# Output projection with tokens on the partitions, in a two-layer encoder with window and differential attention

## The chip, the core and the metric

The kernel runs on one core of one Trainium2 chip. The metric is the time of one execution on the device in microseconds (us). All matrix work is float32 in the reference; the kernel splits each operand into a high part `hi` (rounded to the matmul type fp32r) and a rest `lo`, and makes one product out of three: hi·hi, lo·hi and hi·lo.

## The reference

Two sequences pass through the same two layers: 1024 prompt tokens and 512 sample tokens, each with 16 meta tokens in front, so 1040 and 528 tokens, 1568 in all, of D = 1024 values. A layer is (cut, with `rmsnorm(x, g) = x * rsqrt(mean(x*x) + EPS) * g`):

```
def layer(x, cos, sin, w_in, w_out, pre_g, post_g, ...):
    h = rmsnorm(x, pre_g)
    aq, ak, av, ag, bq, bk, bv, bg = split(h @ w_in)        # 3328 columns
    oa = window_gqa_attention(rope(aq), rope(ak), av, sink) * silu(ag)   # 512 wide
    ob = rmsnorm(diff_attention(rope(bq), rope(bk), bv, lam), subln_g) * (1 - lambda_init) * silu(bg)   # 512 wide
    o = concat([oa, ob]) @ w_out                            # 1024 x 1024
    return x + rmsnorm(o, post_g)
```

After the second layer the meta tokens are cut off; 1536 tokens go out.

## The kernel before

Everything lies with the model's dimension on the partitions ("dims on partitions"): x, the normed h and the projections are tiles of 128 dims by tokens. The 1568 tokens are cut into four chunks of 392 (`CH`); `dense` multiplies a stationary 128x128 block of weights by the 392 tokens of a chunk and adds up over the depth in a PSUM tile `ps_d`, of which there are two. The attention output ("mix") goes to DRAM as `MX` and comes back in halves of 512 dims: half `FH` is complete early (window attention), the other only at the layer's end.

Every operation is first recorded and then placed on its engine's queue by a list scheduler (`schedule`, L329). It has cost constants of its own and a priority for each operation, which is its number in the program less a boost and a base. So the order on an engine is not the order of the code, and nearly all instructions carry the line of the helper that emits them (L451). An operation written as `any_copy` or `any_tt` goes to the engine that the scheduler finds free first.

The output projection of layer l (`outproj`, L1306) runs in steps that a string per layer lists (`O0`, `O1`; a letter, then chunks):

- `b` (`first`): load the early half of mix (`load_mix`, which also splits it into hi and lo), multiply by half of `w_out`, copy the results from PSUM to `part`. It lies beside attention.
- `s` and `S` (`second`): the other half; VectorE adds `ps_d` to `part`, ScalarE squares the sums, and the squares are added up over the eight blocks of 128 dims (`squares`).
- `f` (`fetch`): load x. `p` (`post`): inverse root of the mean square (`rstd_bc`), post gain, residual sum, store to `X1` (layer 0) or to the output. In layer 0 also the statistics of the new x (`prestats`).
- `n` (`pre`, `prenorm`): pre gain times x times inverse root, split in hi and lo, which is the input `hT` of layer 1's projection (`inproj`, `project`).

With dims on the partitions a sum over dims crosses partitions. `rstd_bc` (L693) does it so: TensorE transposes the sums of squares into a `ps_t` tile, VectorE reduces along the free axis into a small tile `sm`, GpSimd makes the power −1/2 there, and TensorE spreads `sm` over 128 partitions by a second transpose, from which a copy makes `rb` [128 x tokens]:

```
nc.tensor.transpose(pt[0:m, 128 * j:128 * j + 128], acc[:, o:o + m], ident)
...
nc.gpsimd.tensor_tensor(col[0:m, ja:jb], col[0:m, ja:jb], mhalf[0:m, ja:jb], op=ALU.pow)
...
nc.tensor.transpose(pb[:, o:o + m], col[0:m, j:j + 1].to_broadcast([m, 128]), ident[0:m, 0:m])
```

Names in the rows: `ps_d` is the PSUM tile of dense products, `ps_s` of scores, `ps_o` of value products, `ps_t` of transposes; `whl` is a weight split in hi and lo (some lie in `vv` or `kk`, pools of attention that are free by then), `slot` and `pp` are large working tiles (mix, part, x, h), `ru`, `t`, `at` smaller ones.

Of the kernel before, what the change touches and what calls it, by code (L numbers as in the profile page):

```python
# [21 lines left out]
D = 1024  # L22
# [10 lines left out]
ICH = [[(0, 392)], [(392, 392)], [(784, 256), (1056, 120)], [(1176, 392)]], [[c] for c in CH]  # L33
OCH = [
    [[c] for c in CH],
    [[(16, 384)], [(400, 384)], [(784, 256), (1056, 128)], [(1184, 384)]],
]
SEQ = [(0, LP), (LP, LS)]
# [6 lines left out]
O0 = "b0123 f1 S01 s23 f0 p0 p1 n0 f2 p2 f3 n1 n2 p3 n3"  # L45
O1 = "b0123 s0 s2 s1 f1 s3 f2 f0 p1 p2 p0 f3 p3"
# [6 lines left out]
STORE = ((2, 2, 2, 2), (4, 4, 2, 1))  # L53
# [5 lines left out]
PRE_ACT = ((0, 0, 0, 0, 0, 0, 0, 0), (1, 1, 1, 1, 1, 1, 1, 1))  # L59
POST_ACT = ((0, 0, 0, 0, 0, 0, 0, 0), (1, 0, 1, 0, 1, 0, 1, 0))  # L60
# [67 lines left out]
PE_SWITCH = 0.39  # L128
POOL_MAX = 300
# [109 lines left out]
class Recorder:  # L239
# [89 lines left out]
    def schedule(self):  # L329
# [16 lines left out]
        def push(o):  # L346
            for e in o.alts:
                heapq.heappush(ready[e], (o.prio, o.seq, o))
# [194 lines left out]
def hymba_kernel(ctx, tc, xT, w_in, w_out, rope, masks, pre_g, post_g, sub_g, sink_b, sink_m, lam_in, yT):  # L543
# [97 lines left out]
    postg = const.tile([128, NL, 8], F32, name="postg")  # L641
    dma(postg, post_g)
# [33 lines left out]
    X1 = dr.tile([128, 8, T], F32, name="X1")  # L676
# [75 lines left out]
    def prenorm(l, ci, xs, rb, n):  # L752
        his, los = [], []
        for i in range(2):
            hi, lo = pair(F32R)
            for j in range(4):
                r = slice(j, j + 1)
                h = at_p([128, 1, CN])
                scaled(h, xs[i][:, r], preg[:, l, 4 * i + j:4 * i + j + 1], rb, n, PRE_ACT[l][2 * ci + i])
# [10 lines left out]
    def load_w(src, pool=None, pri=0):  # L770
        nc.boost = BOOST_W + pri * 100000
        nc.extra = [after[0]] if pool and after else []
        raw = (p_p if pri else wraw_p)([128, 1024])
# [71 lines left out]
    def project(l, e, w, ci, early):  # L845
# [5 lines left out]
        if l == NL - 1 and ci == 0 and k in ("aq1", "aq2", "gate"):  # L851
            segs = [(META, segs[0][1] - META)]
            hi, lo = [x[:, META:] for x in hi], [x[:, META:] for x in lo]
# [432 lines left out]
    def load_mix(l, ci, half, small=False):  # L1286
# [3 lines left out]
        n = sum(m for _, m in OCH[l][ci])  # L1290
        for r0 in range(4 * half, 4 * half + 4, k):
            hi, lo = [p_p([128, 2, CN], F32R) for _ in range(2)] if small else pair(F32R)
            o = 0
            nc.extra = [after[0]] if small else []
            for (t0, m) in OCH[l][ci]:
                dma(lo[:, :, o:o + m], SC[l]["MX"][r0:r0 + k, :, t0:t0 + m].rearrange("e p t -> p e t"))
                o += m
# [6 lines left out]
        return rows(his, k), rows(los, k), n  # L1304

    def outproj(l):  # L1306
        part, mix, accs, kept = {}, {}, {}, {}
        src = xT.rearrange("(a p) t -> p a t", p=128) if l == 0 else X1
        dst = X1 if l == 0 else yT.rearrange("(a p) t -> p a t", p=128)

        def first(*cs_):
            for ci in cs_:
                mix[ci] = load_mix(l, ci, FH[l])
                part[ci] = pair()
# [10 lines left out]
        begun = {}  # L1325

        def squares(ci, d, od, n):
            acc = accs[ci][0]
            if d == 0:
                nc.scalar.activation(acc[:, 0:n], od, AF.Square)  # L1330
                begun[ci] = nc.last
            else:
                nc.extra = [begun[ci]]
                sq = ru_p([128, 2, CN])[:, 0]
                nc.scalar.activation(sq[:, 0:n], od, AF.Square)
                nc.extra = []
                nc.any_tt(acc[:, 0:n], acc[:, 0:n], sq[:, 0:n], ALU.add)

        def second(*cs_, keep=True):
            for ci in cs_:  # L1340
                mix[ci] = load_mix(l, ci, 1 - FH[l], ci == 3)
                accs[ci] = t1_p([128, CN]), mix[ci][2]
            for dp in range(4):
# [4 lines left out]
                else:  # L1348
                    w = kept[dp]
                for ci in cs_:  # L1350
                    hi, lo, n = mix[ci]
                    for d in (2 * dp, 2 * dp + 1):
                        ps = dense(wrows(w, 4 * (d % 2), 4), hi, lo, n, keep and SPARE[1])
                        od = part[ci][d // 4][:, d % 4, 0:n]
                        nc.boost = BOOST_S
                        nc.vector.tensor_tensor(od, od, ps[:, 0:n], op=ALU.add)
                        nc.boost = 0
                        squares(ci, d, od, n)

        def full(*cs_):  # L1360
            for ci in cs_:
                hb, lb, n = load_mix(l, ci, FH[l])
                ha, la, n = load_mix(l, ci, 1 - FH[l], ci == 3)
                mix[ci] = ha + hb, la + lb, n
                part[ci] = pair()
                accs[ci] = t1_p([128, CN]), n
            for dp in range(4):
                wa = load_w(w_out[l, 1 - FH[l], dp], k_p if dp % 2 else None)
                wb = load_w(w_out[l, FH[l], dp], v_p if dp % 2 else None)
                for ci in cs_:  # L1370
# [153 lines left out]
```

## Time and profile before

| | |
|---|---|
| runs of the kernel before | 1966.04, 1966.86, 1968.27 us; median 1966.86 |
| the profiled execution | 1966.48 us; span from first to last instruction 1964.5 us |
| mean granted clock of TensorE | 0.978 of full speed |
| TensorE busy | 1839.0 us, 94% of the span |
| VectorE busy | 1551.5 us, 79% |
| ScalarE busy | 1013.2 us, 52% |
| GpSimd busy | 272.8 us, 14% |

The busy share is a mean over stages with different limits: a stage may be bound by an engine that has the smaller share over the span. The DMA engines moved 271 MB in the span, at a mean of 138 GB/s.

### The profile page before, as it was taken

The numbers are of one execution on the slowest core, as the hardware profiler recorded it, in microseconds if no ns is written. First come the engines' busy times: TensorE is split into PE (matmuls) and PEld (weight loads), VectorE is DVE, ScalarE is ACT, GpSimd is POOL, SyncE is SP. The second block draws the span as 40 slices with busy tenths as digits, with TensorE's granted clock in tenths as the row PEclk, the third lists the DMA queues.
The fourth block names the chain that finished last, engine by engine and source line by source line (L and its number), as shares of the span: only waits on it lengthen the run. The fifth ranks groups of instructions, "written<-read, shape, count | busy, mean of one in ns | idle before, by whom it ended". The sixth has DMA issues, their size and how long they took to land. (4 is left out here: it accounts for less than half of the span.)

```text
span 1964.5 us, 33387 instructions
## 1 busy us (share of the span) xinstructions
PE 1839.0 (94%) x11424; PEld 1751.8 (89%) x11424; DVE 1551.5 (79%) x3384; ACT 1013.2 (52%) x2364; POOL 272.8 (14%) x486
## 2 busy tenths in 40 slices
PE   6999999999999999999687999999999999999995
PEld 5989999999989989998576999999999999889995
DVE  8858788888787797698898596887868859768778
ACT  4335445454454465576445354554545538658642
POOL 3001211211112110010121021011111101100010
PEclk8999999999999999999798999999999999999998
DMA  7253363434443765555343436344463475674444
GB/s 248 58 158 104 113 175 109 135 114 124 139 124 94 165 163 151 134 151 149 133 158 97 151 93 180 99 140 138 109 182 93 120 182 127 168 204 98 127 157 152
DMA packets 289011, 271.05 MB, mean 138 GB/s; under 512 B 91402, under 2 KB 266058, under 8 KB 288714
## 3 DMA queue, kind: packets, MB, share of 16 engines
q1 hardware_dynamic: 288842, 268.92, 48.9%
q8 instruction: 91, 1.49, 0.3%
q14 instruction: 78, 0.64, 0.1%
HBM read 147.43 MB, written 95.94 MB: 124 GB/s over the span
## 5 line engine op out<-in xcount | busy, mean ns | idle before, releaser
L451 PE MATMUL ps_d<-slot,whl 128*128 128x392 f32 (+2 forms) x5712 | 1176.7, 348 | 29.7 <-DVE slot L451 15.4
L451 PEld LDWEIGHTS ps_d<-slot,whl 128*128 128x128 f32 x5712 | 995.6, 191 | 44.4 <-DVE slot L451 19.6
L451 PE MATMUL ps_s<-kk,qq 128*128 128x264 f32 (+9 forms) x1496 | 284.5, 318 | 21.1 <-ACT pp L451 5.4
L451 PE MATMUL ps_o<-at,vv 128*128 128x256 f32 (+6 forms) x1368 | 286.6, 308 | 11.3 <-DVE og L451 4.3
L451 ACT ACTIVATE pp<-ps_s,sm 116x1040 f32<-116x1040 f32 (+4 forms) x208 | 203.8, 980 | 159.7 <-DVE sm L451 152.7
L451 DVE TENSOR_TENSOR at<-ps_t,at 128x256 fp32r<-128x256 f32 (+6 forms) x472 | 224.2, 481 | 71.3 <-ACT at L451 65.1
L451 ACT ACTIVATE at<-ps_t 128x256 fp32r<-128x256 f32 (+9 forms) x435 | 187.8, 440 | 178.4 <-PE ps_t L451 167.3
L451 PEld LDWEIGHTS ps_s<-kk,qq 128*128 128x128 f32 (+4 forms) x1496 | 227.3, 184 | 48.6 <-ACT pp L451 9.6
L451 DVE TENSOR_REDUCE sm<-ps_s 116x1 f32<-116x1040 f32 (+4 forms) x208 | 218.5, 1051 | 43.4 <-PE ps_s L451 42.1
L451 ACT ACTIVATE pp<-pp,sm 128x336 f32<-128x336 f32 (+5 forms) x339 | 200.7, 606 | 85.0 <-DVE sm L451 83.5
L451 PEld LDWEIGHTS ps_o<-at,vv 128*128 128x128 f32 (+1 forms) x1368 | 214.8, 190 | 22.7 <-DVE at L451 7.5
L451 PE MATMUL ps_t<-ident,pp 128*128 128x128 f32 (+4 forms) x1208 | 192.8, 269 | 3.9 <-DVE at L451 2.7
L451 POOL TENSOR_TENSOR pad<-pp,pad 128x64 fp32r<-128x64 f32 (+3 forms) x143 | 47.2, 332 | 790.9 <-ACT pad L451 487.4
L451 PEld LDWEIGHTS ps_t<-ident,pp 128*128 128x128 f32 (+4 forms) x1208 | 142.0, 136 | 16.6 <-DVE at L451 2.6
L451 POOL TENSOR_TENSOR sm<-sm 128x2 f32<-128x2 f32 (+3 forms) x112 | 53.1, 475 | 477.9 <-DVE sm L451 464.4
L451 DVE CUSTOM_DVE_ANT_0 pp<-ps_s,mk,nsinks 128x336 f32<-128x336 f32 (+2 forms) x192 | 97.8, 526 | 17.1 <-PE ps_s L451 15.4
L451 ACT ACTIVATE og<-ps_o 64x128 f32<-64x128 f32 (+4 forms) x248 | 65.9, 287 | 57.8 <-PE ps_o L451 34.2
L451 DVE TENSOR_TENSOR slot<-slot 128x784 f32<-128x784 f32 (+8 forms) x74 | 83.7, 1146 | 7.3 <-ACT slot L451 7.0
L451 DVE TENSOR_TENSOR whl<-wraw,whl 128x1024 fp32r<-128x1024 f32 x62 | 76.5, 1234 | 5.4 <-ACT whl L451 5.0
L451 POOL TENSOR_SCALAR sm<-sm 128x2 f32<-128x2 f32 (+6 forms) x72 | 51.8, 720 | 190.7 <-DVE sm L451 185.8
L451 ACT ACTIVATE pad<-pp 128x64 fp32r<-128x64 f32 (+5 forms) x144 | 33.4, 236 | 82.8 <-DVE pp L451 79.2
L451 ACT ACTIVATE ru<-ps_d 128x392 f32<-128x392 f32 (+3 forms) x93 | 45.6, 490 | 57.6 <-PE ps_d L451 49.3
(145 smaller groups left out, 2055.8 us busy)
## 6 DMA issues: line engine op xcount, KB each, us to landing
wraw<-in_w_in_dram SPq DMA_DIRECT2D x48, 512.0 KB
BS<-st SPq DMA_DIRECT2D x112, 196.0 KB
qq<-qq SPq DMA_DIRECT2D x144, 128.0 KB
qq<-AQ SPq DMA_DIRECT2D x96, 128.0 KB
BV<-st SPq DMA_DIRECT2D x28, 392.0 KB
wraw<-in_w_out_dram SPq DMA_DIRECT2D x20, 512.0 KB
slot<-in_x_dram SPq DMA_DIRECT2D x12, 784.0 KB
GT<-ru SPq DMA_DIRECT2D x48, 196.0 KB
```

The costliest lines, as they stand in the source:

```text
L451: fn(*[_real(a) for a in args], **{k: _real(a) for k, a in kw.items()})
```

## The change

The roles in the output projection's matmuls are swapped. A tile of 128 tokens of mix becomes the stationary operand, and 256 columns of `w_out` move; the result has 128 tokens on the partitions and output dims along the free axis. There are 12 such tiles of 128 tokens (`TILES`, three per chunk of 384), and in layer 0 a thirteenth of 80 rows, "chunk 4", with the two sets of 16 meta tokens and 48 tokens that fill it up; its first half waits in DRAM (`PM`).

What follows works on token tiles: ScalarE squares two halves of 512 with a running sum (`stat`), VectorE adds the two sums, GpSimd makes the power of that one column, the post gain is a multiplication by a tile that holds `post_g` on all partitions (`gains`, step `g`), and the residual sum takes the inverse root as a per-partition scalar. `X1`, the second input `xr` and the output lie token by token in DRAM. For layer 1 the normed x of four token tiles is transposed by TensorE block by block into `ps_t`; `any_copy` with the pre gain makes `hi` from it, and a VectorE operation makes `lo`, both straight from PSUM. `rstd_bc` and `prestats` serve only layer 0's first norm now, `squares` and `full` go. Layer 1's chunks start at token 16, and the meta tokens come last (`ICH[1]`). The step strings change, and with them the order.

```
-O0 = "b0123 f1 S01 s23 f0 p0 p1 n0 f2 p2 f3 n1 n2 p3 n3"
-O1 = "b0123 s0 s2 s1 f1 s3 f2 f0 p1 p2 p0 f3 p3"
+O0 = "b01234 f01 S01 g l2 p0 l3 p1 s4 s2 n0 s3 f4 p4 f2 p2 n1 f3 p3 n2 n3"
+O1 = "b0123 g f0 s0 p0 f1 s1 p1 f2 s2 p2 f3 s3 p3"
...
+        def product(ps, c0, w, m, c, M, behind=()):
+            hi, lo = m
+            for r in range(4):
+                nc.extra = list(behind) if r == 0 else []
+                with nc.macro():
+                    for i, (wt, mt) in enumerate(((0, hi), (1, hi), (0, lo))):
+                        nc.tensor.matmul(
+                            ps[0:M, c0:c0 + 256], lhsT=mt[r][:, c:c + M], rhs=w[:, wt, 2 * r:2 * r + 2],
+                            start=(r == 0 and i == 0), stop=(r == 3 and i == 2))
...
             for dp in range(4):
                 w = load_w(w_out[l, FH[l], dp])
+                u, c0 = dp // 2, 256 * (dp % 2)
                 for ci in cs_:
-                    hi, lo, n = mix[ci]
-                    for d in (2 * dp, 2 * dp + 1):
-                        ps = dense(wrows(w, 4 * (d % 2), 4), hi, lo, n)
+                    for j, (c, M) in enumerate(token_tiles(ci)):
+                        ps = ps_d([128, 512])
+                        product(ps, 0, w, mix[ci], c, M)
                         nc.boost = BOOST_E
-                        nc.any_copy(part[ci][d // 4][:, d % 4, 0:n], ps[:, 0:n])
+                        if ci < 4:
+                            nc.any_copy(part[ci][u][:, j, c0:c0 + 256], ps[:, 0:256])
+                        else:
+                            ev = ru_p([128, 256])
+                            nc.any_copy(ev[0:M], ps[0:M, 0:256])
+                            dma(PM[:, 256 * dp:256 * dp + 256], ev[0:M])
...
-        def squares(ci, d, od, n):
-            acc = accs[ci][0]
...
+            def add(od, ps):
+                nc.boost = BOOST_S
+                nc.vector.tensor_tensor(od, od, ps, op=ALU.add)
+                nc.boost = 0
+
+            if keep:
+                for ci in cs_:
+                    for j, (c, M) in enumerate(token_tiles(ci)):
+                        for u in range(2):
+                            ps = ps_d([128, 512])
+                            w = [get(2 * u + x) for x in range(2)]
+                            done = product(ps, 0, w[0], mix[ci, 1], c, M)
+                            product(ps, 256, w[1], mix[ci, 1], c, M, [done])
+                            add(outs(ci, u, j, M), ps[0:M])
+                        norm(ci, j, M)
...
+        def stat(parts, M):
+            r = sm_p([128, 4])
+            for u, p in enumerate(parts):
+                sq = ru_p([128, 512])
+                nc.scalar.activation(sq[0:M], p, AF.Square, scale=1.0 / 32, accum_out=r[0:M, u:u + 1])
+            nc.vector.scalar_tensor_tensor(
+                r[0:M, 2:3], r[0:M, 0:1], EPS, r[0:M, 1:2], op0=ALU.add, op1=ALU.add)
+            nc.gpsimd.tensor_tensor(r[0:M, 3:4], r[0:M, 2:3], mhalf[0:M, 0:1], op=ALU.pow)
+            return r[0:M, 3:4]
...
-            rb = rstd_bc(acc[:, 0:n], n, 1.0 / D)
-            for u in range(2):
-                for a in (0, 2):
-                    t = oo[u][:, a:a + 2]
-                    scaled(t, t, postg[:, l, 4 * u + a:4 * u + a + 2], rb, n, POST_ACT[l][2 * ci + u])
...
+            for j, (c, M) in enumerate(token_tiles(ci)):
+                for u in range(2):
+                    od, x = outs(ci, u, j, M), xv(ci, u, j, M)
+                    nc.any_tt(od, od, late[0][0:M, u], ALU.mult)
+                    nc.vector.scalar_tensor_tensor(x, od, rs[ci, j], x, op0=ALU.mult, op1=ALU.add)
...
+                if l < NL - 1:
+                    r = stat([xv(ci, u, j, M) for u in range(2)], M)
+                    for u in range(2):
+                        nc.any_copy(xv(ci, u, j, M), xv(ci, u, j, M), r)
...
-                prenorm(l + 1, ci, xin[ci], rbs[ci], accs[ci][1])
...
+                for k in range(4):
+                    d = slice(128 * k, 128 * k + 128)
+                    pt = ps_t([128, 512])
+                    with nc.macro():
+                        for x in range(4):
+                            i = 3 * ci + x
+                            M = 128 if i < 12 else 80
+                            h = xv(i // 3, u, i % 3, M)[:, d]
+                            nc.tensor.transpose(pt[:, 128 * x:128 * x + M], h, ident[0:M, 0:M])
+                    g = preg[:, l + 1, 4 * u + k:4 * u + k + 1]
+                    p = pt[:, 8 * ci:8 * ci + CN]
+                    nc.any_copy(hi[:, k], p, g)
+                    nc.vector.scalar_tensor_tensor(lo[:, k], p, g, f32(hi[:, k]), op0=ALU.mult, op1=ALU.subtract)
```

The first place is TensorE's queue between layer 0's attention and layer 1's first score (`kk`). Before, the last stretch of it is

```order
L451 MATMUL ps_t<-ident,t_10852 98x128 x4
L451 MATMUL ps_d<-slot,whl 128x392 x15
L451 MATMUL ps_t<-ident,sm 128x98 x4
L451 MATMUL ps_d<-pp,whl 128x392 x12
L451 MATMUL ps_t<-ident,slot 98x128 x4
L451 MATMUL ps_d<-pp,whl 128x392 x12
L451 MATMUL ps_t<-ident,sm 128x98 x4
L451 MATMUL ps_d<-pp,whl 128x392 x24
L451 MATMUL ps_d<-slot,kk 128x392 x24
```

After the change the queue behind the last value product (`ps_o`) begins so:

```order
L451 MATMUL ps_o<-at,vv 128x512
L451 MATMUL ps_d<-whl,slot 128x256 x12
L451 MATMUL ps_t<-ident,slot 128x128 x12
L451 MATMUL ps_d<-whl,slot 128x256 x30
L451 MATMUL ps_t<-ident,slot 128x128 x8
L451 MATMUL ps_d<-whl,slot 128x256 x15
L451 MATMUL ps_t<-ident,slot 128x128 x8
L451 MATMUL ps_d<-whl,slot 128x256 x3
L451 MATMUL ps_d<-kk,at 80x256 x12
```

The transposes of `t` and `slot` (sums of squares) and of `sm` (spreading), each with products between, are gone there; transposes of normed tiles (`slot`), 8 to 12 in a row, stand between narrow products of the same projection. In the whole stretch from the last value product to the first score there are 543 wide matmuls and 72 transposes before, and 252 narrow and 399 wide matmuls and 144 transposes after; 249 wide ones stand behind the last transpose of the last chunk, where 150 stood.

The second place is the end of VectorE's queue. Before, its last rows are

```order
L451 SCALAR_TENSOR_TENSOR slot<-slot,postg,rb 128x384 x2
L451 TENSOR_TENSOR slot<-slot,ps_d 128x384 x2
L451 TENSOR_TENSOR slot<-slot 128x4x384
L451 TENSOR_TENSOR t_22663<-t_22663,ru 128x384 x2
L451 TENSOR_REDUCE sm<-ps_t 128x3
L451 TENSOR_TENSOR slot<-slot,rb 128x384 x4
L451 TENSOR_TENSOR slot<-slot 128x384 x4
L451 SCALAR_TENSOR_TENSOR slot<-slot,postg,rb 128x384 x4
L451 TENSOR_TENSOR slot<-slot 128x384 x4
```

and after the change

```order
L451 TENSOR_TENSOR slot<-slot,ps_d 128x512 x2
L451 SCALAR_TENSOR_TENSOR sm<-sm 128x1
L451 TENSOR_TENSOR slot<-slot 128x512
L451 SCALAR_TENSOR_TENSOR slot<-slot,sm 128x512 x2
L451 TENSOR_TENSOR slot<-slot 128x512
L451 TENSOR_TENSOR slot<-slot,ps_d 128x512
L451 SCALAR_TENSOR_TENSOR sm<-sm 128x1
L451 TENSOR_TENSOR slot<-slot 128x512
L451 SCALAR_TENSOR_TENSOR slot<-slot,sm 128x512 x2
```

Behind the last sum with `ps_d` there stand a column addition, a product with the gain (the other half's stands before it or on another engine) and two residual operations of one token tile, where four rows of a whole chunk stood behind a reduction.

## Rows read from the trace of the kernel before

**Rows 1.** The page's busy times: us, share of the span, instructions.

```profile
PE 1839.0 (94%) x11424; PEld 1751.8 (89%) x11424; DVE 1551.5 (79%) x3384; ACT 1013.2 (52%) x2364; POOL 272.8 (14%) x486
```

**Rows 2.** Windows: stretch, length, busy of PE, PEld, DVE, ACT, POOL; clock, DMA.

```profile
897.40:950.40 53.00, 49.41 (x294) 45.86 (x295) 45.42 (x125) 35.79 (x102) 5.38 (x12) 0.94 0.45 130
950.40:1079.00 128.60, 93.81 (x457) 85.44 (x456) 116.88 (x199) 66.05 (x110) 26.27 (x18) 0.84 0.41 135
1079.00:1106.70 27.70, 27.70 (x161) 27.33 (x161) 10.47 (x16) 6.09 (x10) 0.00 (x0) 1.00 0.66 204
1845.00:1855.00 10.00, 9.79 (x69) 9.12 (x69) 9.01 (x34) 8.94 (x28) 1.38 (x3) 1.00 0.48 152
1869.70:1945.20 75.50, 71.27 (x400) 67.75 (x399) 59.81 (x104) 28.05 (x55) 7.28 (x7) 1.00 0.48 159
1945.20:1964.50 19.30, 1.97 (x8) 1.00 (x6) 12.34 (x23) 1.48 (x3) 1.04 (x2) 0.60 0.38 139
```

**Rows 3.** Waits of TensorE, 950.4 to 1079: total us, times, longest.

```profile
PE ps_t L451 <- POOL sm L451: 21.4, 5, 10.5
PE ps_d L451 <- DVE slot L451: 9.8, 7, 3.7
```

**Rows 4.** VectorE's groups by shape, 897.4 to 1079: busy, mean ns | idle before.

```profile
L451 DVE SCALAR_TENSOR_TENSOR slot<-slot,postg,rb 128x392 f32<-128x392 f32 x32 | 19.0, 631 | 2.7 <-ACT rb L451 2.7
L451 DVE TENSOR_TENSOR slot<-slot 128x784 f32<-128x784 f32 x20 | 18.8, 966 | 0.1
L451 DVE TENSOR_TENSOR slot<-at,slot 128x392 fp32r<-128x392 f32 x32 | 17.2, 557 | 0.1
...
L451 DVE TENSOR_TENSOR slot<-slot,ps_d 128x392 f32<-128x392 f32 x28 | 15.2, 555 | 4.1 <-PE ps_d L451 3.3 <-PE ps_o L451 0.7
L451 DVE TENSOR_TENSOR t<-t,ru 128x392 f32<-128x392 f32 x25 | 13.9, 558 | 0.5 <-ACT ru L451 0.3
...
L451 DVE TENSOR_TENSOR slot<-slot 128x1568 f32<-128x1568 f32 x4 | 7.1, 1784 | 0.0
L451 DVE TENSOR_REDUCE sm<-ps_t 98x4 f32<-98x512 f32 x8 | 5.5, 685 | 3.0 <-PE ps_t L451 2.9
...
L451 DVE SCALAR_TENSOR_TENSOR rw<-ps_d,scl,cs 128x392 f32<-128x392 f32 x4 | 2.5, 621 | 0.3 <-PE ps_d L451 0.3
...
L451 DVE TENSOR_TENSOR at<-ps_t,at 128x256 fp32r<-128x256 f32 x2 | 0.8, 424 | 0.0
```

**Rows 5.** TensorE's timeline at two places: start, us, operation, xcount.

```profile
926.35 0.69 PE L451 MATMUL ps_o<-at,vv 128*128 128x256 f32 x4
926.87 0.70 PE L451 MATMUL ps_d<-slot,whl 128*128 128x392 f32 x3
...
996.20 4.53 PE L451 MATMUL ps_d<-pp,vv 128*128 128x392 f32 x24
1000.58 2.92 PE L451 MATMUL ps_d<-slot,whl 128*128 128x392 f32 x15
...
1845.53 1.03 PE L451 MATMUL ps_t<-ident,pp 128*128 128x128 f32 x8
1846.32 1.29 PE L451 MATMUL ps_d<-slot,whl 128*128 128x384 f32 x6
...
1850.10 0.63 PE L451 MATMUL ps_o<-at,vv 128*128 128x256 f32 x4
1850.57 0.44 PE L451 MATMUL ps_t<-ident,pad 128*80 128x128 f32 x4
```

**Rows 6.** Timeline of the end, all engines: start, us, operation [idle before].

```profile
1940.92 4.48 PE L451 MATMUL ps_d<-pp,vv 128*128 128x384 f32 x24 [0.32 <-DVE slot L451]
...
1946.09 0.99 ACT L451 ACTIVATE ru<-slot 128x384 f32<-128x384 f32 x2 [4.19 <-DVE slot L451]
...
1951.24 0.85 POOL L451 TENSOR_TENSOR sm<-sm,mhalf 128x3 f32<-128x3 f32 x1
...
1959.48 1.96 DVE L451 TENSOR_TENSOR slot<-slot 128x384 f32<-128x384 f32 x4
```

More of the change, by code (lines that the diff above doesn't have):

```diff
@@ L675, in hymba_kernel @@
     nc.base = 0
-    X1 = dr.tile([128, 8, T], F32, name="X1")
+    X1 = dr.tile([T, D], F32, name="X1")
+    PM = dr.tile([80, D], F32, name="PM")
     SC = []
@@ L772, in load_w @@
         nc.extra = [after[0]] if pool and after else []
-        raw = (p_p if pri else wraw_p)([128, 1024])
+        raw = (p_p if pri or pool and after else wraw_p)([128, 1024])
         dma(raw, src)
@@ L1347, in second @@
                         kept[dp] = w
-                else:
[L1349 to L1358, printed above, removed]
@@ L1409, in pre @@
-        def pre(ci):
-            if l < NL - 1:
-                prenorm(l + 1, ci, xin[ci], rbs[ci], accs[ci][1])
-        steps = dict(b=first, s=second, S=lambda *c: second(*c, keep=False), F=full, f=fetch, p=post, n=pre)
+                    return w
+                return kept[dp]
+            def add(od, ps):
[12 more added lines that the diff above has]
+                        norm(ci, j, M)
+            else:
+                for dp in range(4):
+                    w = get(dp)
+                    for ci in cs_:
+                        for j, (c, M) in enumerate(token_tiles(ci)):
+                            ps = ps_d([128, 512])
+                            product(ps, 0, w, mix[ci, 1], c, M)
+                            add(outs(ci, dp // 2, j, M)[:, 256 * (dp % 2):256 * (dp % 2) + 256], ps[0:M, 0:256])
+                            if dp == 3:
+                                norm(ci, j, M)
@@ new lines, in norm, with fetch @@
+        def norm(ci, j, M):
+            rs[ci, j] = stat([outs(ci, u, j, M) for u in range(2)], M)
+        xin = {}
+        def fetch(ci):
+            nc.boost = BOOST_M if ci == 4 else 0
+            if ci == 4:
+                nc.extra = [after[0]]
+                xm = p_p([128, 2, 512])
+                o = 0
+                for (t0, m) in OCH[ci]:
+                    dma(xm[o:o + m].rearrange("p u d -> p (u d)"), src[t0:t0 + m])
+                    o += m
+                nc.extra = []
+                xin[ci] = [xm]
+            else:
+                if l == 0 and ci == 3:
+                    xin[ci] = [p_p([128, 2, 512]) for _ in range(3)]
+                else:
+                    xin[ci] = halves([128, 3, 512])
+                nc.extra = [after[0]] if l == 0 and ci == 3 else []
+                for u in range(2):
+                    for j, t0 in enumerate(TILES[ci]):
+                        dma(xv(ci, u, j), src[t0:t0 + 128, 512 * u:512 * u + 512])
+                nc.extra = []
+            nc.boost = 0
@@ L1414, in outproj @@
+        steps = dict(b=first, s=second, S=lambda *c: second(*c, keep=False), f=fetch, p=post, n=pre, l=load, g=gains)
         for step in OUT_ORDER[l].split():
             nc.base = BASE[l].get(step[0], 0)
-            steps[step[0]](*[int(c) for c in step[1:]])
+            for c in ([step[1:]] if step[0] in "bsS" else step[1:] or [""]):
+                steps[step[0]](*[int(x) for x in c])
         nc.base = 0
```

153 lines of the change are left out of this document (71 added, 82 removed).

## The prediction

> **What bounds the kernel now.** I first read the busy shares of the page: TensorE is busy 94% of the span and no other engine is above 79% [rows 1]. So a saving on another engine counts only where TensorE is seen to wait, and the next view to read is busy time by stretch. I cut stretches at marks of the program: the last unit of attention of layer 0 (897.4 to 950.4 us), the turn from there to the last lo part of layer 1's input (950.4 to 1079), the input projection up to layer 1's first score product (1079 to 1106.7), and at the end layer 1's second half of the output projection (1869.7 to 1945.2) and what follows its last matmul (1945.2 to 1964.5) [rows 2].
>
> [...] In the turn TensorE is busy 93.8 us of 128.6, and VectorE 116.9: VectorE is the fuller engine there. [...] And the last 19.3 us hold 8 matmuls: a chain, in which VectorE works 12.3 us. The waits of TensorE in the turn say which: 21.4 us for the small GpSimd tile `sm` (the inverse root, before it is spread over 128 partitions by a transpose), and 9.8 us for VectorE's work on `slot` [rows 3].
>
> How much VectorE work is at stake is read from its groups between 897.4 and 1079 [rows 4]. Seven of them belong to the part that is rewritten, and so do 32 pre-gain products on `at`, as long as the 32 lo operations.
>
> **The change, part by part.** *TensorE.* A 392-wide matmul costs 0.1825 us where 24 follow each other: (1000.58 - 996.20)/24 [rows 5]. For a 256-wide one there are two rows, both of four in attention: 0.1175 (1850.57 - 1850.10) and 0.13 (926.87 - 926.35). The wide rate scaled by columns gives 0.119, which lies at the lower one; I take 0.119 and keep 0.13 as the upper bound, 0.1175 as the lower. A 128x128 transpose costs 0.099 us, (1846.32 - 1845.53)/8.
> - Layer 0: 768 matmuls of 392 columns become 13 token tiles x 96 = 1248 of 256 (the thirteenth tile is the 80 meta and filler tokens): 1248 x 0.119 - 768 x 0.1825 = 148.5 - 140.2 = +8.3 us; about half of it in the first halves under attention, +4.
> - Layer 1: 768 of 384 columns become 1152 of 256: 137.1 - 137.3, nothing. Its input projection has new chunks; 288 matmuls for queries and gates are 16 columns narrower: 288 x 16/392 x 0.1825 = -2.1 us.
> - Transposes: 88 for the norms go (the order lists them), 128 come: +40 x 0.099 = +4.0 us; the 24 that go from the end save 2.4 there, the rest lies in the turn.
>
> *VectorE in layer 0.* By the means of [rows 4] this goes: 32 post-gain products x 0.631, 16 residual sums x 0.966, 28 sums of squares x 0.558, the squares of the new x (1.784 + 0.966 + 0.557 for each of four chunks), eight reductions x 0.685, 64 pre-gain and lo operations x 0.557, 32 sums with PSUM x 0.555: 123 us. This comes: 24 sums with PSUM of 256 (0.424), 20 of 512 (about 0.69, by the slope of 0.409 us between the 392- and the 784-wide sum), 26 gain products of 512 (0.68), 26 residual operations (0.631 + 120 x 0.00104 = 0.76), 32 lo operations from PSUM (0.621), ten hi parts (0.62), and about 10 us of small columns, scaled copies and the fifth chunk: 97 us. Net -26 us. The squares go to ScalarE with a running sum; it is busy 102 us of the 181.6 there [rows 2] and loses its own pre-gain pass, so I cost that at nothing; without that cover each 512-wide square would delay its tile's norm by under 1 us.
>
> *The turn.* VectorE has 162.3 us of work in 181.6 us (897.4 to 1079), 89%. With 136 us at the same 89% the last lo part comes after 153 us, 28.6 earlier. But the new order leaves 249 wide matmuls of the input projection behind the last transposes, 249 x 0.1825 = 45.4 us, where now 27.7 us are left: net -11 us. The other bound is TensorE alone: from attention's last product to the first score it has 252 narrow and 399 wide matmuls and 144 transposes, 30.0 + 72.8 + 14.3 = 117.1 us, for what now takes from 950.4 to 1106.7, 156.3 us: -39. I take -17, near the VectorE end, because VectorE stays the engine that the norms wait for; a little beyond it, because the eight trips TensorE - GpSimd - TensorE go, and with them the 21.4 us in which TensorE stood with ready products behind a transpose.
>
> *Where the stall goes.* VectorE, not TensorE, now waits for `sm`: one column per token tile on GpSimd, 26 times in layer 0. Behind a residual operation that waits stand the sums that free `ps_d`. In the order other tiles' sums stand between, so I add nothing, and this is rival B.
>
> *Narrow products and PSUM.* With half of the depth and 256 columns a `ps_d` tile is full after 12 x 0.119 = 1.43 us instead of 12 x 0.1825 = 2.19, and there are two of them. An eviction costs VectorE 0.424 and must come within that time although VectorE and ScalarE also serve attention. I add 2 us; the bounds are 0 and 10.
>
> *The end.* Now 19.1 us lie between the last dense matmul (1940.92 + 4.48) and the end: sum, squares, transposes, the power on GpSimd, transposes, copy, sixteen VectorE operations of a quarter chunk each, the last at 1959.48 to 1961.44, and 3.1 us for its store [rows 6]. After the change the last matmul is followed by one 512-wide sum (0.69), one square (0.99/2 for 384, so 0.65 for 512) with its running sum (estimate 0.2), a one-column addition (0.2), the power (at most the 0.85 of three columns), two residual operations (1.4) and the store (3.1), with five hand-overs of about 0.2: 8 us. That is -11.
>
> *Sum.* Turn -17, end -11, first halves +4, input projection -2, transposes at the end -2 (inside the -11 chain only in part; I count 1), evictions +2: -25. The profiled run took 1966.5 us (span 1964.5 and 2.0 around it), 0.4 below the median of the runs shown, so this holds for both: **1941 us**.
>
> **Rivals.** *A, TensorE becomes the bound of the turn.* For it: no engine has more than 136 us of work left in what are now 181.6 us, and the waits behind `sm` on TensorE are gone. Against it: 89% is what the fuller engine reaches now. Then -39 instead of -17: 1919.
> *B, the turn gives nothing.* The 26 us come back as VectorE waits on the one-column chain, square, addition, power, and as filled `ps_d`. For it: TensorE waits for VectorE's `slot` already now [rows 3]. Then only the end counts: 1958.
> *C, the narrow products cost more.* Place: all 2400 of them, about 2150 outside the turn's hidden part. At 0.13 the gain is gone by 2150 x 0.011 = 24: 1965, no change. From 0.131 on the kernel is slower, at 0.14 it takes 1986. For it: one of two rows stands at 0.13. Against: the other stands at 0.1175, and the wide rate gives 0.119 by columns alone.
> [...]
> *That the change does nothing* would need C's rate or a turn and an end that both keep their length; I know no row for the second.
>
> **How the numbers follow.** Forecast (1930 to 1952) 0.54; A, 0.15; B (1952 to 1962) 0.18; no change, C at its bound, 0.05; C beyond it 0.04; D 0.04. About 0.2% is what a measurement of this kernel can tell from no change, 3.9 us. Faster: 0.54 + 0.15 + 0.18 = 0.87; same 0.05; slower 0.08. The range for 8 in 10 leaves out no change and both slower cases (0.13) and half of A (0.07): 1920 to 1960.
>
> **What the profile after would show.** VectorE's busy time between the last unit of attention and the last lo part 26 us shorter, and the turn's waits of TensorE for `sm` gone. 256-wide `ps_d` matmuls 0.119 us apart in runs of 12 and more; at 0.13 C is right. [...] First score of layer 1 about 17 us sooner after attention's last product than the 156.3 us of now. Last matmul to end 8 us. I am wrong if VectorE shows new idle time before `slot<-slot,sm`, or `ps_d` waits for ScalarE and VectorE grow under attention by more than 10 us.

## The result and the profile after

The changed kernel takes 1938.49 us (median of four runs, 1930.33 to 1938.88), before it was 1966.45 over the runs on the same chips; the ratio is 0.9852, with a 95% interval of 0.982 to 0.9884. Run again beside the last experiments (e9) it gave 0.9839 (0.9825 to 0.9854); e9's numbers leave out one execution of five, which took 2986 us at a granted clock of 0.56. Forecast were 1941 us, 25 less than before; measured are 28 less. The profiled run took 1938.61, with a span of 1936.8.

The page's busy times after, as in [rows 1]:

```profile
PE 1843.4 (95%) x12328; PEld 1771.3 (91%) x12328; DVE 1515.2 (78%) x3363; ACT 1008.1 (52%) x2417; POOL 279.3 (14%) x516
```

TensorE has 904 more instructions and 4 us more busy time in a span that is 28 us shorter, and VectorE 36 us less. To see where the time went I cut both traces at the same four marks of the program, all read from TensorE's timeline: the start of layer 0's last value product, layer 1's first score product, layer 1's last value product, the end.

| us | to last value product, layer 0 | turn to first score | layer 1 to last value product | to the end | span |
|---|---|---|---|---|---|
| before | 950.1 | 156.6 | 762.8 | 95.0 | 1964.5 |
| after | 960.8 | 136.5 | 749.9 | 89.5 | 1936.8 |
| difference | +10.7 | -20.1 | -12.9 | -5.5 | -27.7 |

The stretches of the changed kernel in windows, columns as in [rows 2]: the last 55 us of layer 0's attention, the first 16.8 us of the turn, the 7 us behind them, the rest up to the last lo part of layer 1's input, the input projection up to the first score, and what follows the last matmul's start.

```profile
905.80:960.80 55.00, 49.94 (x392) 46.84 (x391) 49.91 (x144) 40.69 (x115) 9.82 (x13) 1.00 0.47 130
960.80:977.60 16.80, 4.73 (x28) 3.60 (x26) 14.56 (x33) 11.02 (x27) 7.20 (x9) 0.70 0.67 220
977.60:984.60 7.00, 5.84 (x25) 5.55 (x26) 5.93 (x7) 3.92 (x6) 0.00 (x0) 0.50 0.81 250
984.60:1068.20 83.60, 82.21 (x578) 80.75 (x577) 69.79 (x131) 45.24 (x92) 14.80 (x20) 1.00 0.44 133
1068.20:1097.30 29.10, 29.10 (x172) 28.96 (x171) 5.48 (x9) 5.26 (x10) 0.00 (x0) 1.00 0.62 187
1928.30:1936.80 8.50, 0.28 (x3) 0.07 (x1) 4.06 (x8) 0.72 (x2) 0.92 (x1) 0.81 0.33 123
```

The turn is now two things. For 16.8 us TensorE does almost nothing (4.7 us busy), and the granted clock falls from 1.00 to 0.50 between 967.4 and 967.6. It is still 0.50 in the next 7 us, where 25 narrow products keep TensorE busy for 5.84 us, 0.23 us each; from 984.6 on TensorE is busy 82.2 of 83.6 us at a clock of 1.00, and VectorE, the fuller engine before, 69.8. VectorE's work from 905.8 to 1068.2 is 140.2 us (49.9 + 14.6 + 5.9 + 69.8), where 162.3 stood in [rows 2].

TensorE's waits from 960.8 to 1068, as in [rows 3]:

```profile
PE ps_t L451 <- ACT slot L451: 7.6, 1, 7.6
PE ps_t L451 <- DVE slot L451: 3.5, 1, 3.5
PE ps_d L451 <- DVE slot L451: 1.2, 1, 1.2
PE ps_d L451 <- ACT slot L451: 1.0, 1, 1.0
```

No wait for `sm` is left on TensorE; these four lie in the first 19 us, and the rest of the list adds up to 1.4. VectorE's groups from 905.8 to 1068.2 that took the place of those in [rows 4]:

```profile
L451 DVE SCALAR_TENSOR_TENSOR slot<-ps_t,preg,slot 128x392 fp32r<-128x392 f32 x32 | 19.1, 620 | 3.6 <-ACT slot L451 3.5
L451 DVE TENSOR_TENSOR slot<-slot 128x512 f32<-128x512 f32 x24 | 16.4, 706 | 0.1
L451 DVE SCALAR_TENSOR_TENSOR slot<-slot,sm 128x512 f32<-128x512 f32 x18 | 13.6, 773 | 0.7 <-POOL sm L451 0.7
...
L451 DVE TENSOR_TENSOR slot<-slot,ps_d 128x512 f32<-128x512 f32 x12 | 8.2, 683 | 1.6 <-PE ps_d L451 1.4
L451 DVE TENSOR_TENSOR slot<-slot,ps_d 128x256 f32<-128x256 f32 x16 | 6.6, 414 | 0.7 <-PE ps_d L451 0.7
```

The durations are within 4% of those that were worked out (in the order of the lines 0.621, 0.68, 0.76, 0.69, 0.424), and VectorE waits for `sm` 0.7 us in all. Narrow products in a run and, in the last two lines, wide ones of the input projection, TensorE's timeline, as in [rows 5]:

```profile
993.75 1.58 PE L451 MATMUL ps_d<-vv,slot 128*128 128x256 f32 x12
995.16 1.93 PE L451 MATMUL ps_d<-kk,slot 128*128 128x256 f32 x15
996.93 0.51 PE L451 MATMUL ps_d<-vv,slot 128*128 128x256 f32 x3
...
1068.99 0.70 PE L451 MATMUL ps_d<-slot,kk 128*128 128x392 f32 x3
...
1077.03 0.70 PE L451 MATMUL ps_d<-slot,vv 128*128 128x392 f32 x3
```

(996.93 - 995.16)/15 is 0.118 us for each narrow one; between the last two lines 45 wide ones begin, (1077.03 - 1068.99)/45 = 0.179 us for each, a little under the 0.1825 of [rows 5]. The end, all engines, as in [rows 6]:

```profile
1927.00 1.58 PE L451 MATMUL ps_d<-vv,pp 128*128 128x256 f32 x12
...
1929.51 0.68 DVE L451 TENSOR_TENSOR slot<-slot,ps_d 128x512 f32<-128x512 f32 x1
1930.28 0.63 ACT L451 ACTIVATE ru<-slot 128x512 f32<-128x512 f32 x1 [3.00 <-DVE slot L451]
...
1931.27 0.92 POOL L451 TENSOR_TENSOR sm<-sm,mhalf 128x1 f32<-128x1 f32 x1 [3.73 <-DVE sm L451]
1932.23 1.41 DVE L451 SCALAR_TENSOR_TENSOR slot<-slot,sm 128x512 f32<-128x512 f32 x2 [0.44 <-POOL sm L451]
```

From the end of the last matmul (1927.00 + 1.58) to the end of the span are 8.2 us, where 19.1 stood: one sum, one square, one column through the power, two residual operations, and the store.

### The profile page after: what moved, and what is told of

It is laid out like the page before. It is cut to its first block, busy times and chain, and to the rows that moved or that the text cites. A ratio compares the mean times of both kernels' runs of the same rounds, so it can differ in the third digit from the quotient of the medians.

```text
span 1936.8 us, 35552 instructions
## 1 busy us (share of the span) xinstructions
PE 1843.4 (95%) x12328; PEld 1771.3 (91%) x12328; DVE 1515.2 (78%) x3363; ACT 1008.1 (52%) x2417; POOL 279.3 (14%) x516
## 4 chain that ended last, share of the span: by engine, by line
PE 70%; DVE 11%; DMA 8%; ACT 4%; issue 4%; SPq 2%; POOL 1%; DVEq 0%; POOLq 0%; ACTq 0%
PE ps_d L451 43%; PE ps_s L451 10%; PE ps_o L451 9%; PE ps_t L451 8%; DVE at L451 2%; DVE pp L451 2%; DVE slot L451 2%; ACT pp L451 2%; SPq L451 2%; DVE sm L451 1%; DMA vv<-BV 1%; DVE og L451 1%; DMA kk<-AK 1%; DVE ru L451 1%; POOL sm L451 1%
## 5 line engine op out<-in xcount | busy, mean ns | idle before, releaser
L451 PE MATMUL ps_d<-slot,whl 128*128 128x392 f32 (+2 forms) x4560 | 938.2, 347 | 15.0 <-ACT slot L451 6.7
L451 PEld LDWEIGHTS ps_d<-slot,whl 128*128 128x128 f32 x4560 | 785.7, 190 | 22.2 <-ACT slot L451 6.7
L451 PE MATMUL ps_d<-whl,slot 128*128 128x256 f32 x1800 | 259.0, 288 | 8.6 <-DVE slot L451 6.0
L451 PEld LDWEIGHTS ps_d<-whl,slot 128*128 128x128 f32 x1800 | 235.1, 192 | 14.3 <-DVE slot L451 7.2
L451 ACT ACTIVATE pp<-pp,sm 128x336 f32<-128x336 f32 (+6 forms) x347 | 206.6, 607 | 61.0 <-DVE sm L451 57.6
L451 PEld LDWEIGHTS ps_o<-at,vv 128*128 128x128 f32 (+1 forms) x1368 | 214.0, 190 | 16.8 <-ACT pp L451 5.4
L451 PE MATMUL ps_t<-ident,pp 128*128 128x128 f32 (+6 forms) x1248 | 203.5, 269 | 3.1 <-DVE at L451 1.6
L451 PEld LDWEIGHTS ps_t<-ident,pp 128*128 128x128 f32 (+6 forms) x1248 | 147.8, 137 | 14.7 <-ACT pp L451 2.8
L451 DVE CUSTOM_DVE_ANT_0 pp<-ps_s,mk,nsinks 128x336 f32<-128x336 f32 (+2 forms) x192 | 97.1, 528 | 22.1 <-PE ps_s L451 20.3
L451 POOL TENSOR_TENSOR sm<-sm,mhalf 128x1 f32<-128x1 f32 (+7 forms) x98 | 80.8, 830 | 132.9 <-DVE sm L451 129.6
L451 ACT ACTIVATE ru<-ps_d 128x392 f32<-128x392 f32 (+5 forms) x100 | 48.7, 487 | 73.9 <-PE ps_d L451 64.2
L451 DVE TENSOR_TENSOR slot<-slot 128x512 f32<-128x512 f32 (+3 forms) x79 | 73.9, 945 | 8.4 <-ACT slot L451 8.0
```

Of the source, the lines that this page charges most:

```text
L451: fn(*[_real(a) for a in args], **{k: _real(a) for k, a in kw.items()})
```

## What TensorE waits for at the turn's start

Three lists of the changed kernel belong together. TensorE's timeline:

```profile
961.05 1.59 PE L451 MATMUL ps_d<-whl,slot 128*128 128x256 f32 x12
962.47 0.38 PE L451 MATMUL ps_t<-ident,slot 128*128 128x128 f32 x2
970.42 1.59 PE L451 MATMUL ps_t<-ident,slot 128*128 128x128 f32 x6 [7.57 <-ACT slot L451]
975.50 1.09 PE L451 MATMUL ps_t<-ident,slot 128*128 128x128 f32 x4 [3.49 <-DVE slot L451]
977.60 0.79 PE L451 MATMUL ps_d<-whl,slot 128*128 128x256 f32 x2 [1.01 <-ACT slot L451]
```

the queue that issues the transfers:

```profile
968.73 0.37 SPq L451 DMA_DIRECT2D MX<-og  x1
...
971.08 0.37 SPq L451 DMA_DIRECT2D slot<-MX  x1
971.56 0.44 SPq L451 DMA_DIRECT2D pp<-PM  x1
972.11 1.08 SPq L451 DMA_DIRECT2D pp<-in_w_out_dram  x2
```

and ScalarE's split of the chunk of mix:

```profile
976.06 1.48 ACT L451 ACTIVATE slot<-slot 128x1536 fp32r<-128x1536 f32 x1 [1.28 <-DMA slot<-MX]
```

By name TensorE waits for the norm of a token tile, whose transposes stand at the head of its queue. But the products behind those transposes were not ready either: the last attention result goes to DRAM at 968.7, 7.9 us after its product began, comes back as a chunk of mix from 971.1 on, and the product at 977.6 waits for ScalarE to split it, which ends at 977.5. I call this idle time of TensorE the stand. Two quarters of `w_out` (`pp<-in_w_out_dram`) are asked for only at 972.1, because these loads wait for the last store. The kernel before stood at the same place:

```profile
950.70 2.92 PE L451 MATMUL ps_d<-slot,whl 128*128 128x392 f32 x15
964.11 0.91 PE L451 MATMUL ps_t<-ident,sm 98*128 98x98 f32 x4 [10.50 <-POOL sm L451]
964.73 0.68 PE L451 MATMUL ps_d<-pp,whl 128*128 128x392 f32 x1
```

and ScalarE split the chunk for that last product just ahead of it:

```profile
962.77 0.84 ACT L451 ACTIVATE pp<-pp 128x784 fp32r<-128x784 f32 x1
```

The 10.50 us before 964.11 are half of the 21.4 us that [rows 3] puts down to `sm`. But the split ended only at 963.6, so for all but 0.5 us of them the product behind the transposes was not ready either. The runs e3, e9 and e10 below bear on this.

## Experiments

In each, the rest of the kernel is as before or as changed. Ratios are to the kernel before on the same chip, with 95% intervals. All of them are built by the same list scheduler, so an edit also moves other instructions.

**e1, e2: one layer old, one new.**

```
-        outproj(l)
+        (outproj_b, outproj)[l](l)        # e1: layer 0 old, layer 1 new, residual from xr
+        (outproj, outproj_b)[l](l)        # e2: layer 0 new, layer 1 old, residual from xT
```

> Layer 0 keeps the old output projection and norms (and layer 1 the old chunks), layer 1 has the new ones; layer 1 takes its residual from the kernel's input x instead of layer 0's result, which leaves out one dependency and no work. By stretches of the two traces layer 1's part of the change is 5.5 us after its last value product and 8.5 us ahead of it (12.9 less the 4.4 us of dense work that the new chunks save there). If both belong to layer 1's own steps: 14 us under before, about 1953. If what layer 1 gained under attention came with layer 0's chunks, only 5.5 us: about 1961.

> Layer 0 has the new output projection and norms, layer 1 the old ones, with its residual from the kernel's input x. By stretches layer 0's part is +10.7 us before its last value product, -20.1 in the turn and -4.4 by the new chunks: 14 us under before, about 1953. If layer 1's gain under attention came with layer 0's chunks too: 22 us under, about 1944. The two kernels' gains should add up to the 28 of the whole.

e1 took 1959.52 us, 0.9953 (0.9932 to 0.9974); e2 1943.93, 0.9884 (0.9866 to 0.9903). The gains, 0.47% and 1.16%, add up to 1.63%, the whole change's 1.48% within its interval. They fall nearer to the second expectations. By the four marks:

| us | to last value product, layer 0 | turn | layer 1 to last value product | to the end | span |
|---|---|---|---|---|---|
| e1 | 952.1 | 158.2 | 755.8 | 92.1 | 1958.2 |
| e2 | 960.7 | 136.9 | 758.9 | 85.1 | 1941.6 |

Layer 1's own steps (e1 against before, last two stretches) are worth 762.8 + 95.0 - 755.8 - 92.1 = 9.9 us. In e2 layer 1 has the old steps and is still 762.8 + 95.0 - 758.9 - 85.1 = 13.8 us shorter than before: that came with layer 0's new steps and the new chunks of layer 1's input. Much of it lies early: from the first to the 129th score product of layer 1 there are 121.2 us before, 120.9 in e1, 111.8 in e2 and 112.3 in the changed kernel, 9 us less, ahead of any output projection of layer 1. Not all of that is gained: 27 wide products fewer stand in this stretch (351 where 378 stood, 4.8 us at 0.179), 15 of them now ahead of the first score and 12 behind the 129th. TensorE's idle time in it falls from 3.3 to 0.6 us in the changed kernel.

**e3, e4: the kernel before, without the trip, and with less VectorE work.** e3 leaves out the inverse roots of layer 0's two norms, e4 most of a product with one:

```
-            rb = rstd_bc(acc[:, 0:n], n, 1.0 / D)
+            rb = rstd_bc(acc[:, 0:n], n, 1.0 / D) if l else spread(acc[:, 0:n], n)   # e3: a copy; the same in prestats
...
+                    nc.scalar.activation(h[:, 0, 0:n], xs[i][:, j, 0:n], AF.Copy, scale=g)            # e4
+                    nc.vector.tensor_tensor(h[:, 0, 0:8], h[:, 0, 0:8], rb[:, 0:8], op=ALU.mult)
```

> The kernel before, in which layer 0's two inverse roots per chunk are left out: rb is a copy of the sums of squares themselves, so the transposes, the reduction, the power and the spreading transposes go (64 transposes, eight reductions), and VectorE's other work stays. If VectorE's load bounds the turn, only its 5.5 us of reductions count: about 1960. If it is the trip TensorE - GpSimd - TensorE behind which ready products stand, the 21.4 us of waits for sm go: 1945 or below.

> The kernel before, in which the pre-gain step of layer 1's input multiplies by the inverse root only 8 of 392 columns (the dependence stays, the rest of that product is left out): 32 x about 0.45 = 14 us less VectorE work in the turn, the trips stay. If VectorE's load bounds the turn: 12 to 14 us under before, about 1953. If the trips do: within 4 us of before.

e3 took 1953.94 us, 0.9931 (0.9907 to 0.9956), between its two expectations; its turn is 139.4 us, while its last value product comes at 955.9, 5.8 later than before. e4 took 1952.88, 0.9926 (0.9911 to 0.9942); its turn is 143.2. The turn of e3 in a window, and TensorE's waits in it:

```profile
955.90:1067.50 111.60, 80.70 (x399) 75.01 (x398) 110.88 (x191) 65.54 (x109) 3.46 (x4) 0.88 0.48 156
```

```profile
PE ps_d L451 <- ACT pp L451: 13.2, 1, 13.2
PE ps_d L451 <- DVE slot L451: 11.2, 6, 7.5
```

The same of e4:

```profile
949.70:1065.20 115.50, 88.41 (x460) 81.46 (x459) 107.57 (x211) 60.89 (x99) 19.67 (x18) 0.88 0.45 147
```

Without the trip VectorE works 110.9 of 111.6 us: it is the bound of the old turn, and the trips only added some 12 us in which it stood (128.6 - 116.9 in [rows 2]). In e4 the trips are left. The cut product takes VectorE 3.7 us instead of 17.0; 4.3 of these 13.3 us come back as operations that the scheduler then gave to VectorE. With 9.0 us less busy time of VectorE the turn is 13.4 us shorter (156.6 - 143.2). And without any trip TensorE still stands 13.2 us at the place of the 10.50, now for the split of mix (`ACT pp`), and its waits from the last value product to the first score add up to 30.7 us, where 34.6 stood before. So the trip covered another wait of about the same length.

**e5, e6: the changed kernel with more work for one engine.**

```
+                        nc.vector.tensor_tensor(od, od, od, op=ALU.max)      # e5, layer 0, behind the gain
...
+                            for _ in range(2):                               # e6
                                 nc.tensor.transpose(pt[:, 128 * x:128 * x + M], h, ident[0:M, 0:M])
```

> The changed kernel with one more 512-wide VectorE operation (a maximum of the tile with itself, which changes nothing) for each half of each token tile in layer 0, behind the product with the gain: 26 x 0.68 = 17.7 us more VectorE work, about 14 of them in the turn. In the trace of the changed kernel VectorE works 90 of the turn's 107 us, TensorE stands 15 us at its start and then hardly. If VectorE still bounds the turn: 14 us over the changed kernel, a ratio to before of 0.992. If TensorE does now, behind that one gap: at most 4 us, 0.987.

> The changed kernel with each transpose of a normed tile issued twice: 128 x 0.099 = 12.7 us more TensorE work, of which the 32 of chunk 0 lie in the gap at the turn's start and 96 behind it. If TensorE bounds the turn now: 9.5 us over the changed kernel, ratio to before 0.990. If VectorE does: at most 3 us, 0.987.

e5 took 1955.86 us, 0.9932 (0.991 to 0.9955); e6 1958.91, 0.9945 (0.9924 to 0.9966). By the expectations one of the two additions should have been nearly hidden; neither was. For e6 that agrees with a turn bound by TensorE: its turn is 153.1 us, 16.6 more, of which 12.7 are the transposes and 2.1 are 12 more products of the input projection (12 x 0.179). The rest of its loss lies outside the turn: 2.6 us up to the last value product, and layer 1, which takes 751.9 + 2.1 = 754.0 us with these products added back, instead of 749.9. For e5 it is less plain. Its last value product comes 4.7 us later, though VectorE has only 3 more 512-wide products and maxima ahead of it (14 where 11 stood; in the turn 38 where 15 stood); 9 narrow products more stand there (1.1 us). In the turn 51 wide products more stand ahead of the first score, 9.1 us, so that 153.2 - 9.1 + 1.1 - 136.5 = 8.7 us are longer. TensorE's idle time in the turn is 22.3 us, where 14.6 stood; its longest wait at the start is 11.8 us now, and further on e5's windows are, columns as in [rows 2]:

```profile
984.00:1020.00 36.00, 35.81 (x287) 35.41 (x286) 34.98 (x64) 21.75 (x50) 8.52 (x8) 0.96 0.56 186
1020.00:1050.00 30.00, 24.98 (x144) 23.43 (x143) 26.74 (x53) 18.95 (x39) 6.16 (x8) 0.94 0.39 119
```

VectorE is busy 35.0 of 36 us, and in the 30 us behind them TensorE stands 5. So the added work took up the slack that VectorE has in the changed kernel (69.8 of 83.6 us), and beyond it VectorE is a bound again. And layer 1, which has none of the added work, takes 746.1 + 9.1 = 755.2 us instead of 749.9. e7, e8 and e12, which have the same order of TensorE's instructions in layer 1 as e5, show 753.0 to 754.5 by the same sum, while the changed kernel profiled again (e9) shows 747.8. So 3 to 7 us of e5's loss are the order that the scheduler fell into, and some 12 lie ahead of layer 1, 8.7 of them in the turn.

**e7, e8: the last attention result first.**

```
+        nc.boost = 3000                       # e7, e8: from the copy out of ps_o to the store in MX
...
+            for y in range(0, k, 2 if l == 0 and half == 0 and ci in (2, 3) else k):      # e8: load and split by twos
```

> The changed kernel, in which the operations that bring an attention result from PSUM to DRAM go ahead of all others on their engines (a boost of 3000). In the changed kernel's trace TensorE stands at the turn's start until the last attention result has gone to DRAM and come back as a chunk of mix: 7.7 us from the last value product to its store, because ScalarE and VectorE put norm work between. If that way sets the gap: 3 to 4 us off the gap. If the norms of the first token tiles do (their transposes stand at the head of TensorE's queue): no change or 1 us more.

> As the run before, and the late half of mix of chunks 2 and 3 in layer 0 is loaded and split in two pieces of two heads instead of one of four, so that products can begin on the first piece. If the way of the last attention result sets the gap: another 2 us off it, 5 to 6 in all, ratio to before about 0.983. If the norms do: as the changed kernel, 0.985.

e7 took 1944.92 us, 0.9876 (0.9845 to 0.9908); e8 1945.55, 0.9877 (0.9841 to 0.9913): no gain. From the last value product to the next product that follows the stand there are 15.0 us in e7 (966.66 to 981.66) and 15.7 in e8, instead of 16.8; the store comes 6.1 us after that product in e7 and 8.4 in e8, instead of 7.9. The way was shortened by less than forecast in e7 and its first part not at all in e8, and layer 1's order (3 to 7 us, as in e5) and a last value product that comes 6 us later ate it. Inconclusive as to the rest.

**e9, e10, e11: what the stand is worth.** e9 is the changed kernel again, for the chip. In e10 the loads that waited for the last attention result's store wait for its last value product only:

```
+            read[:] = [nc.last]               # behind the last value product
...
-        nc.extra = [after[0]] if pool and after else []
+        nc.extra = [read[0]] if pool and after else []        # and at the four other places
...
-BASE = ({'f': 400, 'p': 100, 's': -100, 'S': 0, 'b': 800}, {'f': 0, 'S': 400})
+BASE = ({'f': 400, 'p': 0, 's': -100, 'S': 0, 'b': 800}, {'f': 0, 'S': 400})       # e11 alone
```

> The changed kernel itself, on the chip of the three runs that follow, so that they can be held against it: ratio to before 0.985, as measured first. No theory differs on it.

> The changed kernel, in which the loads that were held back until the last attention result is stored (two quarters of w_out's late half into attention's freed buffers, the meta tokens' first half, x of the meta tokens and of chunk 3; in layer 1 the last chunk of mix) wait only for the last value product. Nothing is left out. If TensorE's stand at the turn's start is the bound there, and the 120 narrow products of chunk 2 and of the meta tile that wait for those weights can fill it: 14 us of products, less the time that the weights need to come, so 6 to 9 us under the changed kernel, ratio to it 0.996. If the loads only crowd the store of the last attention result, or VectorE, busy there, sets the pace: within 3 us.

> As the run before, and the steps p of layer 0 (gain, residual, statistics) have no priority over the other dense steps, so that VectorE and ScalarE come to the weights first. Nothing is left out. If TensorE's stand is the bound: 8 to 11 us under the changed kernel. If the norms of the first tiles are: 0 to 4 us over it, since they come later.

e9 took 1935.73 us, 0.9839 (0.9825 to 0.9854); e10 1925.12, 0.9795 (0.9779 to 0.9812), which is 10.6 us under e9 by the medians and 8.7 by the ratios, and beats both kernels. e11 took 1934.44, 0.9829 (0.9815 to 0.9844), not the 8 to 11 us less that were expected: its turn, 130.3 us, is nearly as short as e10's, but layer 1 came out in another order and takes 755.6. TensorE's timeline of e10 at the turn's start:

```profile
960.95 1.58 PE L451 MATMUL ps_d<-whl,slot 128*128 128x256 f32 x12
967.45 0.50 PE L451 MATMUL ps_d<-kk,at 128*80 128x256 f32 x1 [4.92 <-ACT kk L451]
969.97 0.72 PE L451 MATMUL ps_d<-kk,at 128*80 128x256 f32 x2 [2.02 <-DVE kk L451]
970.48 0.84 PE L451 MATMUL ps_d<-kk,slot 128*128 128x256 f32 x3
```

The products that need the late quarters of `w_out` (in `kk`) begin at 967.45, where the changed kernel stood till 977.60; these quarters are asked for at 960.6 now. The turn is 128.6 us, e9's is 136.0; TensorE's instructions are the same in number there and in the same order in layer 1, which takes 748.3 and 747.8. So 7.4 us are the stand's; the turns of the two profiles of the changed kernel (136.5 and 136.0) differ by 0.5. The last stretch is 84.7 us instead of 90.5: two quarters of layer 1's `w_out` are asked for at 1837.8, 0.2 us after its last value product, where e9 asks at 1853.6, 9.1 us after it. TensorE's waits for them there (`kk`, 1.7 and 0.9 us) are gone, and the granted clock is 1.00 from 1837.6 to 1914.6, where e9 has 0.96 from 1844.5 to 1926.5.

**e12: without the power.**

```
-            nc.gpsimd.tensor_tensor(r[0:M, 3:4], r[0:M, 2:3], mhalf[0:M, 0:1], op=ALU.pow)
-            return r[0:M, 3:4]
+            return r[0:M, 2:3]
```

> The changed kernel without the powers on GpSimd in the token-tile norms (38 of about 0.85 us; the scale is then the mean square itself). If the one-column chain square, sum, power is a stall (rival B of the prediction): 5 us or more under the changed kernel. If it is covered by other tiles' work except at the very end: 1 us under it, no difference that can be measured.

e12 took 1943.64 us, 0.9879 (0.9864 to 0.9894), 8 more than e9 by the medians. Of these 5 are layer 1's order (as in e5); the turn, less the 9.1 us of products placed ahead of the first score, is 138.9 us, not shorter than e9's 136.0; the last stretch is 3.0 us shorter, of which 1.0 lies behind the last matmul's start (7.5 instead of 8.5 us). The chain over GpSimd costs 1 us at the end; elsewhere no gain shows, though the order moved with the edit, so a small one could be hidden.

## Why the prediction was right, and where it was not

- **Sum.** -25 forecast; -28 in the medians, -27.7 in the spans. The parts were further off than that: +10.7 instead of +6 up to the last value product, -20.1 instead of -17 in the turn, -18.4 instead of -14 behind it. That their misses of +4.7, -3.1 and -4.4 leave under 3 us is luck.
- **First halves +4, evictions +2.** Measured +10.7 up to the last value product. The mis-sized term is "about half of it in the first halves": ahead of that mark TensorE has 996 of the 1248 narrow products (996 x 0.118 = 117.5 us) instead of 609 of the 768 wide ones (609 x 0.179 = 109.0), so 8.5 us fall there, as much as the whole term. The other 2.2 us are idle time of TensorE (54.1 us up to that mark, where 51.9 stood), as much as the evictions were costed.
- **Narrow products at 0.119.** Right, 0.118; rival C falls.
- **The turn, -17.** Measured -20.1, right in size by luck, since the reason was wrong. The step "VectorE stays the engine that the norms wait for" failed: from 984.6 on TensorE is busy 98% of the time and VectorE 83%. Rival A's sum of TensorE's work, 117.1 us, is what the turn holds; to it come some 18 us of the 23.8 up to 984.6, which hold 53 matmuls, 12 of them transposes, or 6 us of work at a clock of 1.00 (41 x 0.118 + 12 x 0.099): the stand, and the products behind it at a clock of 0.50. VectorE's saving was 22.1 us (162.3 - 140.2) where 26 were forecast; that it was the old turn's bound is shown by e3 and e4, and e5 shows that it is not far from a bound in the new one. The clock had no term and is part of the gain: the granted clock is 0.87 on the mean of the old turn and 0.94 of the new one. By an estimate from its mean, about 41 us of the old turn lie at 0.50; in the new one 17 us do (967.5 to 984.6). TensorE is busy 121.8 and 121.9 us although the new turn has 11 us more work at a clock of 1.00 (115.4 and 104.3 by the measured 0.179, 0.118 and 0.099).
- **"The 21.4 us in which TensorE stood with ready products behind a transpose".** Wrong for half of them: in the 10.50 us before 964.11 the next product's input was not ready until 963.6, and e3, which has no such transposes, stands 13.2 us there. That stand, the way of the last attention result through DRAM, stayed in the changed kernel, and it is why the gain ended at -20 and not at A's -39. I had read the name in the list of waits and not what stood behind it in the queue.
- **The input projection, -2.** Measured -9 up to layer 1's 129th score product, in the changed kernel and in e2. Of these 4.8 us are moved and not gained: 15 products more stand ahead of the first score (399, where 384 of the 543 wide ones were the input projection's), which put 2.7 us into the turn, and 12 went behind the mark. The 2.1 us by narrower products lie mostly behind the mark too (30 of the 288 stand ahead of it). Over the whole of layer 1, e2 is 13.8 us shorter with the old steps: 2.7 moved into the turn, 2.1 by narrower products, and 9.0 for which the prediction had no term. TensorE's idle time there falls by 6.3 us (38.9 to 32.6); what made it fall stays open.
- **The end, -11.** 19.1 became 8.2 us, as the chain was summed up; the one column took the power 0.92 us there, where 0.85 was allowed for. The 0.2 us for the running sum, for the column addition and for each of five hand-overs were my estimates without a row. The trace after shows 0.19 for the running sum's read-out, 0.16 for the addition and 0.03 to 0.09 for each hand-over between the last sum with `ps_d` and the residual operations, and 0.93 us from the last matmul's end to that sum, while VectorE is at other work until 1929.58. Of layer 1 as a whole, its own steps are worth 9.9 us in e1. Only 2.9 of them show in the last stretch, since 639 narrow products stand behind the last value product there (75 us) where 381 wide ones stood (67 us), and fewer ahead of it.
- **Rival B, the one-column chain as a new wait.** Does not hold: VectorE waits 0.7 us for `sm` in the whole turn and ScalarE 2.6, and e12 gains 1 us behind the last matmul.
- **Rival D, 0.04, a clock that stays low through the new transposes.** No run shows such a clock. From 984.6 to 1068.2 the granted clock is 1.00, with all but 12 of the transposes of normed tiles in it, in groups of four to eight between products. The stretch at 0.50, from 967.5 to 984.6, begins in TensorE's stand and ends 7 us after it. In e6, where each of these transposes is issued twice, the granted clock is 0.94 on the mean of the turn, as in the changed kernel.

Open stays what the 9.0 us in layer 1 are for which there was no term, and why e5's last value product comes 4.7 us later.

## What to carry to other kernels

A row in a list of waits names the instruction at the head of an engine's queue and what released it; before its time is booked as a gain, look whether the instruction behind it was ready, by the time of its own last input (here a store, a load and a split). When a change relieves the fuller engine of a stage, sum up the next engine's work in that stage as its floor, and add what neither engine sets: 117 us of TensorE and 18 of stand gave the new turn of 136.5. Loads that wait for the end of a phase should wait for the last reader of the buffer that they take, not for the phase's last store: that was 7.4 us in the turn and 6 at the end.

Where a list scheduler sets the order, an edit of one operation can move another stage of the kernel by 3 to 7 us; hold runs against one another by stretches whose order is the same.

## What was not expected of the hardware

The power on GpSimd has no one price by columns. In the changed kernel from 905.8 to 1068.2 one column takes 0.89 us on the mean,

```profile
L451 POOL TENSOR_TENSOR sm<-sm,mhalf 128x1 f32<-128x1 f32 x24 | 21.1, 888 | 29.3 <-DVE sm L451 29.3
```

no less than the 0.85 for three columns in [rows 6]. But that row is the shortest of its kind: over the two traces, before and after, the shortest power of one column on 128 partitions takes 0.53 us, of two 0.69, of three 0.85 and of four (on 98 partitions) 1.01, while the longest of one column takes 2.13. What makes the long ones long no run here shows. And a 512-wide scaling by a per-partition scalar takes VectorE 0.48 us and ScalarE 0.72 (means of 6 and 12 of them in the same stretch).
